# A planned issue order for the output projection and the second layer's input

## Chip, cores and metric

One core of a Trainium2 chip. The metric is the device time of one execution in microseconds (us); lower is better.

## What is computed

Two layers over 256 context rows and 1024 latent rows of width 1024 (1280 rows, ten tiles of 128). Layer 0 is a state-space mixer, layer 1 attention. The change lies at the end of layer 0 and the start of layer 1:

```python
def finish(y, xs, z):
    ...
    return rmsnorm(y * jax.nn.silu(z), norm_w) @ out_w      # 2048 -> 1024
...
h_lat = h_lat + gt[:, None] * o_lat
h_ctx = h_ctx + gtc * o_ctx
...
in_lat = rmsnorm(h_lat, norm_w[i]) * (1.0 + scl[:, None]) + sh[:, None]   # next layer
```

All is float32. A matmul is made of three, with each operand split into a high part that TensorE takes as it is and a low part that is the remainder.

## The kernel before

The kernel runs in stages. The first (the mixer's scans) and the last (attention) are issued by a `Plan`: the code hands it operations, each with its engine, a rank, a duration in us and the buffers that it takes (`hold`); `Plan.order` runs a list schedule over them (each engine takes, whenever it is free, the operation of lowest rank whose inputs and buffers are there), and the operations are then emitted in that order inside `tc.manual_schedule()`, which keeps it. Everything between is emitted in the order of its loops, and the framework's own scheduler, with its own model of time, decides each engine's queue. In the profile, instructions of a later part stand in the queues between those of an earlier one.

The stage of this change, called the output projection here, handles three blocks of token tiles, (0,4), (4,7) and (7,10). For each of 16 slices `kt` of the 2048 inner channels, a block does this:

- SP loads `yt` and `zt` from `y_d` and `z_d` (L1062, L1063; three slots each) and two halves of the weight slice `m_out_w` (L187; six raw slots in `workvv`, the first slice in the ring `wraw`).
- POOL multiplies them (L1064). ACT squares the product (L1068), POOL adds the squares to `acc` (L1069, a tile of `workkl`).
- ACT makes `yh` with the norm weight (L1072), DVE the remainder `yl` (L1073).
- ACT makes `whi` of each weight half (L180); the remainder `wlo` goes to POOL and DVE in turn (L182).
- PE makes six matmuls of 128x512 for each token tile into `po` (L164 to L166): 24 in a slice of block 0, 18 in one of the others. Block 0's first tile has the two `tr` banks of PSUM, all other tiles share the six `ob` banks.

After 16 slices `drain_tile` empties the banks (DVE L992, ACT L993, POOL L994). `closing` finishes the block while the next one runs, a step before each second slice: the sum of squares over channels (PE L1039), the inverse root (DVE L214, POOL L215), and for each token tile the residual sum (DVE L1000, input by SP L999, result to `h1_d` by L1002), its own norm (ACT L1004, L214, L215), the scaling by it (DVE L1007), eight transposes through the `tr` banks (PE L1015), and shift and scale with the split into the second layer's inputs `inh` and `inl` (ACT L1020 and L1026, DVE L1023 and L1027). Block 2's closing runs between the projections of the next stage, which takes it step by step.

What decides which engine makes a weight's remainder, and the order of the loops:

```python
self.n += 1
(G if self.n % 2 else V).tensor_tensor(lo, w, hi.bitcast(FT), op=OP.subtract)
...
for kt in range(16):
    if kt >= 2 and kt % 2 == 0:
        next(after, None)
```

Of the kernel before, what the change touches and what calls it, by code (L numbers as in the profile page):

```python
# [141 lines left out]
def emit(tc, A, out):  # L142
# [92 lines left out]
    def psum(tag, shape):  # L235
        return PS.tile(shape, FT, tag=tag, bufs=PSN[tag], name=tag)
# [735 lines left out]
    with ExitStack() as st:  # L972
# [5 lines left out]
        turn = [-1]  # L978

        def piece():  # L980
            turn[0] += 1
            return raw6[turn[0] % 6]


        rt1 = work[1][0:4, 4]
        inh, inl = both_parts()
        R2 = Ring(S2, 1, 4)

        def drain_tile(t, po):
            h1 = work[0][:, t % 5]  # L990
            g = gts[1 if t < 2 else 0]
            V.tensor_tensor(h1[:, 0:512], po[0], g[:, 0:512], op=OP.mult)  # L992
            S.activation(h1[:, 512:], po[1], AF.Copy)  # L993
            G.tensor_tensor(h1[:, 512:], h1[:, 512:], g[:, 512:], op=OP.mult)  # L994
            return h1

        def residual(t, h1, rstd):
            xt = work[1][:, t % 2]
# [8 lines left out]
            V.tensor_scalar(xt, h1, r, None, op0=OP.mult)  # L1007
            return xt

        def next_input(t, xt):  # L1010
            j = 1 if t < 2 else 0
            for h in range(2):
                p = psum("tr", [128, 4, 128])
                for i in range(4):
                    T.transpose(p[:, i, :], xt[:, (h * 4 + i) * 128:(h * 4 + i + 1) * 128], ident)  # L1015
                w = work[1][:, 2, h * 512:(h + 1) * 512].rearrange("p (a b) -> p a b", a=4)
                for i in range(4):
                    kt = h * 4 + i
                    if i % 2:
                        S.activation(w[:, i], p[:, i], AF.Identity, bias=shcol[1][:, kt, j:j + 1],  # L1020
                                     scale=gcol[1][:, kt, j:j + 1])
                    else:
                        V.tensor_scalar(w[:, i], p[:, i], gcol[1][:, kt, j:j + 1], shcol[1][:, kt, j:j + 1],  # L1023
                                        op0=OP.mult, op1=OP.add)
                ih = inh[:, h * 4:h * 4 + 4, t * 128:(t + 1) * 128]
                S.activation(ih, w, AF.Copy)  # L1026
                V.tensor_tensor(inl[:, h * 4:h * 4 + 4, t * 128:(t + 1) * 128], w, ih.bitcast(FT), op=OP.subtract)  # L1027

        def closing(b0, b1, h1s, acc):

            if b0 == 0:
                c = psum("tr", [128, KT, 4])
                for kt in range(KT):
                    T.transpose(c[:, kt, :], rt1[:, kt * 128:(kt + 1) * 128], ident[0:4, 0:4])
                mod_cols(1, c[:, :, 0:2], c[:, :, 2:4])
            ssq = M2.tile([128, 4], FT, tag="ssy", bufs=2, name="ssy")
            pss = psum("tr", [128, 4])
            for t in range(b0, b1):
                T.matmul(pss[:, t - b0:t - b0 + 1], acc[:, (t - b0) * 128:(t - b0 + 1) * 128], ones[:, 0:1],  # L1039
                         start=True, stop=True)  # L1040
            V.tensor_copy(ssq[:, :b1 - b0], pss[:, :b1 - b0])
            r = rsq(M2, ssq[:, :b1 - b0], 2 * D, "rsy", 2)
            yield
            xn = None
            for t in range(b0, b1 + 1):
                nxt = residual(t, h1s[t], r[:, t - b0:t - b0 + 1]) if t < b1 else None
                if xn is not None:
                    next_input(t - 1, xn)
                xn = nxt
                yield  # L1050

        after = iter(())
        for b0, b1 in ((0, 4), (4, 7), (7, 10)):
            n = (b1 - b0) * 128
            po = {(t, h): psum("ob" if b1 - t < 4 else "tr", [128, 512]) for t in range(b0, b1) for h in range(2)}
            acc = work[1][:, 3, (b0 == 4) * 512:((b0 == 4) + 1) * 512]
            for kt in range(16):
                if kt >= 2 and kt % 2 == 0:
                    next(after, None)
                yt = S2.tile([128, 512], FT, tag=f"yt{(b0 + b0 // 7 + kt) % 3}", bufs=1, name="yt")  # L1060
                zt = S2.tile([128, 512], FT, tag=f"zt{(b0 + b0 // 7 + kt) % 3}", bufs=1, name="zt")
                Q.dma_start(yt[:, :n], y_d[kt, :, b0 * 128:b1 * 128])  # L1062
                Q.dma_start(zt[:, :n], z_d[kt, :, b0 * 128:b1 * 128])  # L1063
                G.tensor_tensor(yt[:, :n], yt[:, :n], zt[:, :n], op=OP.mult)  # L1064
                if kt == 0:
                    S.activation(acc[:, :n], yt[:, :n], AF.Square)
                else:
                    S.activation(zt[:, :n], yt[:, :n], AF.Square)  # L1068
                    G.tensor_tensor(acc[:, :n], acc[:, :n], zt[:, :n], op=OP.add)  # L1069
                yh = S2.tile([128, 512], FR, tag=f"yh{(b0 + b0 // 7 + kt) % 3}", bufs=1, name="yh")  # L1070
                yl = S2.tile([128, 512], FR, tag=f"yl{(b0 + b0 // 7 + kt) % 3}", bufs=1, name="yl")
                S.activation(yh[:, :n], yt[:, :n], AF.Copy, scale=mnw[:, kt:kt + 1])  # L1072
                V.scalar_tensor_tensor(yl[:, :n], yt[:, :n], mnw[:, kt:kt + 1], yh[:, :n].bitcast(FT), op0=OP.mult,  # L1073
                                       op1=OP.subtract)
                if b0 == 0 and kt == 6:
                    for i in range(2):
                        Q.dma_start(rt1[2 * i:2 * i + 2], m_d[:, (i + 1) * 1024:(i + 2) * 1024])
                    for j in range(2):
                        Q.dma_start(gts[j], rows(m_d[j, 0:1024], 128))
                w = [(R2 if kt % 2 and b0 + kt > 1 else WR).load(A["m_out_w"][kt * 128:(kt + 1) * 128, h * 512:(h + 1) * 512],  # L1080
                                                                      piece() if b0 + kt else None)
                     for h in range(2)]
                for t in range(b0, b1):
                    k = slice((t - b0) * 128, (t - b0 + 1) * 128)
                    for h in range(2):
                        mm3(po[t, h], yh[:, k], yl[:, k], w[h][0], w[h][1], kt == 0, kt == 15)
            h1s = {t: drain_tile(t, [po[t, 0], po[t, 1]]) for t in range(b0, b1)}
            for _ in after:
                pass
            after = closing(b0, b1, h1s, acc)  # L1090

# [592 lines left out]
```

## Time and profile before

| | |
|---|---|
| time, median of 3 runs | 2061.88 us (2059.1 to 2063.29) |
| profiled execution | 2048.25 us, span 2046.1 us |
| PE busy | 1970.3 us, 96% of the span |
| DVE, ACT, POOL busy | 69%, 53%, 58% |
| granted TensorE clock, mean | 0.993 |
| output projection | 1025.12 to 1284.54 us of the span |

Engines: PE is TensorE, PEld its weight loads, DVE VectorE, ACT ScalarE, POOL GpSimd, SP SyncE (SPq its queue of DMA issues). A busy share is over the whole span; the stage has its own.

### The profile page before, as it was taken

Reading aid. Unit: us, or ns where it says so; the run is one execution under the profiler, and the core shown is the slowest. Engines: PE = TensorE matmul, PEld = TensorE weight load, DVE = VectorE, ACT = ScalarE, POOL = GpSimd, SP = SyncE. Lnnn points to the kernel's source line nnn. Section 1 sums busy time; section 2 is a strip of 40 time slices with the busy share of each in tenths; the row PEclk is TensorE's granted clock in tenths of the full one; section 3 lists DMA queues with packets and bytes.
Section 4 is the critical chain, followed back from the end, with each engine's and each line's share of the span. In section 5 each row is a group of like instructions: output and inputs, shape, how many; then the busy total and the mean of one; then the engine's idle time right before and its main releaser. Section 6 shows DMA issues by size and latency. Waiting matters only on the chain. (4 is left out here: it accounts for less than half of the span.)

```text
span 2046.1 us, 31950 instructions
## 1 busy us (share of the span) xinstructions
PE 1970.3 (96%) x11352; PEld 1533.5 (75%) x11352; DVE 1411.4 (69%) x1718; ACT 1082.3 (53%) x2004; POOL 1187.8 (58%) x977
## 2 busy tenths in 40 slices
PE   8899999999999999999998989999999999999998
PEld 8778888878887888788876777999786444444476
DVE  1495887787869695866354777755763888888653
ACT  2547768576766767576544555522223445454521
POOL 1202766666657574846287888753443666776722
PEclk9999999999999999999999999999999999999999
DMA  6115555435453546364585665451222011111023
GB/s 240 63 32 142 145 153 166 140 116 165 125 168 98 165 115 183 104 172 141 187 277 165 203 209 180 142 147 32 81 77 92 32 37 42 42 44 41 6 98 108
DMA packets 159699, 249.29 MB, mean 122 GB/s; under 512 B 22106, under 2 KB 57818, under 8 KB 159540
## 3 DMA queue, kind: packets, MB, share of 16 engines
q1 hardware_dynamic: 159252, 246.73, 39.1%
q8 instruction: 89, 1.46, 0.3%
q14 instruction: 70, 0.57, 0.1%
q10 hardware_dynamic: 288, 0.52, 0.1%
HBM read 204.49 MB, written 42.63 MB: 121 GB/s over the span
## 5 line engine op out<-in xcount | busy, mean ns | idle before, releaser
L164 PE MATMUL pj<-inh,whi 128*128 128x512 f32 (+1 forms) x1152 | 439.7, 382 | 3.9 <-DVE dv L449 3.2
L165 PE MATMUL pj<-inl,whi 128*128 128x512 f32 (+1 forms) x1152 | 408.8, 355 | 0.8 <-POOL inl L363 0.8
L166 PE MATMUL pj<-inh,wlo 128*128 128x512 f32 (+1 forms) x1152 | 409.6, 356 | 0.0
L750 POOL TENSOR_SCALAR_AFFINE_SELECT lab<-lab 128x512 f32<-128x512 f32 x160 | 146.6, 923 | 179.7 <-DMA lab<-la_d 168.2
L641 DVE SCALAR_TENSOR_TENSOR acc<-ub,convw,acc 128x1282 f32<-128x1282 f32 x128 | 232.1, 1813 | 18.7 <-ACT acc L638 15.7
L164 PEld LDWEIGHTS pj<-inh,whi 128*128 128x128 f32 x1152 | 218.3, 189 | 33.5 <-DVE dv L449 3.6
L166 PEld LDWEIGHTS pj<-inh,wlo 128*128 128x128 f32 x1152 | 217.5, 189 | 32.1
L165 PEld LDWEIGHTS pj<-inl,whi 128*128 128x128 f32 x1152 | 218.5, 190 | 26.3 <-POOL inl L363 1.2
L1428 POOL TENSOR_TENSOR acc<-acc,P 128x1024 f32<-128x1024 f32 x80 | 192.7, 2408 | 64.9 <-ACT P L1452 63.4
L1452 ACT ACTIVATE P<-sc 128x1024 f32<-128x1024 f32 x160 | 162.9, 1025 | 117.4 <-PE sc L1447 107.5
L756 ACT ACTIVATE W<-lab,u_t 128x128 f32<-128x128 f32 x640 | 201.4, 390 | 36.7 <-POOL lab L750 29.5
L1393 DVE TENSOR_REDUCE mx<-sc 128x2 f32<-128x1024 f32 (+1 forms) x140 | 167.3, 1213 | 55.5 <-PE sc L1272 54.5
L709 POOL TENSOR_TENSOR xw<-xst,te_t 128x256 f32<-128x256 f32 x144 | 141.9, 1002 | 42.4 <-DVE xst L693 16.5
L1463 PE MATMUL ot<-P,vv 128*64 128x512 f32 x640 | 154.7, 605 | 0.0
L1447 PE MATMUL sc<-q,kh 64*128 64x512 f32 x640 | 136.2, 421 | 1.2 <-ACT P L1452 0.9
L598 POOL TENSOR_TENSOR wlo<-wraw,whi 128x512 fp32r<-128x512 f32 x48 | 70.4, 1466 | 107.5 <-ACT whi L595 107.5
L164 PE MATMUL ob<-whi,inh 128*128 128x256 f32 x416 | 119.7, 289 | 3.3 <-DVE mx L1309 3.3
L164 PE MATMUL ob<-whi,yh 128*128 128x512 f32 x288 | 115.5, 405 | 6.5 <-DVE workkh L992 6.5
L166 PE MATMUL ob<-whi,inl 128*128 128x256 f32 x416 | 117.9, 284 | 0.0
L165 PE MATMUL ob<-wlo,inh 128*128 128x256 f32 x416 | 117.8, 284 | 0.0
L166 PE MATMUL ob<-whi,yl 128*128 128x512 f32 x288 | 115.4, 401 | 2.3 <-DVE yl L1073 2.3
L165 PE MATMUL ob<-wlo,yh 128*128 128x512 f32 x288 | 115.4, 401 | 0.0
(275 smaller groups left out, 4576.1 us busy)
## 6 DMA issues: line engine op xcount, KB each, us to landing
lab<-la_d SPq DMA_DIRECT2D x160, 256.0 KB
wraw<-in_w_in SPq DMA_DIRECT2D x96, 256.0 KB
workvv<-in_m_out_w SPq DMA_DIRECT2D x94, 256.0 KB
mraw<-in_mod_w SPq DMA_DIRECT2D x64, 256.0 KB
es<-e_d SPq DMA_DIRECT2D x128, 128.0 KB
spare<-in_mod_w SPq DMA_DIRECT2D x32, 256.0 KB
z_d<-zs SPq DMA_DIRECT2D x32, 256.0 KB
q_d<-qs SPq DMA_DIRECT2D x128, 64.0 KB
```

The costliest lines, as they stand in the source:

```text
L164: T.matmul(o, lh, rh, start=first, stop=False)
L165: T.matmul(o, lh, rl, start=False, stop=False)
L166: T.matmul(o, ll, rh, start=False, stop=last)
L641: V.scalar_tensor_tensor(t["a"], ub[i % 2][:, k:k + CW], convw[:, ct, k:k + 1], t["a"], op0=OP.mult, op1=OP.add)
L709: G.tensor_tensor(t[d], s["xst"][:, c], te_t[:, d, c, h4][:, :, None].to_broadcast([128, 4, 64]), op=OP.mult)
L750: G.affine_select(t["l", d], t["l", d], [[0, 4], [sgn, 128]], OP.is_ge, NEVER, base=0, channel_multiplier=-sgn)
L756: S.activation(t["w", d][:, h], t["l", d][:, h], AF.Exp, bias=u_t[:, d, c, 4 * g + h:4 * g + h + 1])
L1393: V.tensor_reduce(max_place(t["m"][0], i), o, AX.X, OP.max)
L1428: E.tensor_tensor(t[e], t["P", k0] if two else t[e], t["P", kt], op=OP.add)
L1447: T.matmul(o[:, h], (first_row[r] if n == 3 else (kh, kl, kh)[n][r, kv, k]), x[(0, 0, 1, 2)[n]][r], start=(n == 0), stop=(n == 3))
L1452: S.activation(t["P", kt], flat(t["s", kt]), AF.Exp)
L1463: T.matmul(t["o"][h * 64:(h + 1) * 64], vv[:, kt, kv], t["P", kt][:, h * 512:(h + 1) * 512], start=(kt == 0), stop=(kt == NT - 1))
```

## The change

Each operation of the output projection and of the closings of blocks 0 and 1 becomes an operation of a `Plan`, and the whole is emitted inside `tc.manual_schedule()`. Ranks are 1000 for a block and 20 for a slice; loads stand 45 to 50 below their slice, drains 700 below, the sum of squares 400 below; a closing's token tiles stand 60 apart from the next block's start. Block 2's closing stays as it was. The engines of three things change: of the weights' remainders POOL makes half in block 0, as before, and a quarter in blocks 1 and 2 (half before), DVE the rest; and in the planned closings the scaling by the norm goes from DVE to ACT. One PE operation is the six matmuls of a token tile in a slice, and it waits for both weight halves.

```diff
-ANY = ("tc", "wparts", "pj", "sc", "dn")
+ANY = ("tc", "wparts", "pj", "sc", "dn", "tr")
...
+        rings = {n + str(i): 1 for n, k in (("y", 3), ("yh", 3), ("raw", 6), ("h1", 5), ("x2", 2), ("w", 2)) for i in range(k)}
+        plan = Plan({**rings, "wa": 4, "wb": 4, "ob": 6, "tr": 2})
...
+            a = plan.op("SP", bring, [], R - 45, takes=raws)
+            a = plan.op("ACT", high, [a], R - 30, .63, takes=[parts], uses=raws)
+            pool = n % (2 if b == 0 else 4) == 1
+            return t, parts, plan.op(*(("POOL", lambda: low(G), [a], R - 30, 1.6) if pool else ("DVE", lambda: low(V), [a], R - 30, 1.2)),
+                                     uses=[*raws, parts])
...
+            a = plan.op("SP", bring, [], R - 50, us=.76, takes=[hy], move=2 * MOVE)
+            a = plan.op("POOL", lambda: G.tensor_tensor(t["yt"], t["yt"], t["zt"], op=OP.mult), [a], R - 40, 1.47 if wide else 1.27, uses=[hy])
+            h = plan.op("ACT", high, [a], R - 35, .71 if wide else .6, takes=[hh], uses=[hy])
+            l = plan.op("DVE", low, [h], R - 35, 1.3 if wide else 1.1, uses=[hy, hh])
...
+                    last[t] = plan.op("PE", product, [last.get(t), ly] + [w[2] for w in ws], R + t - b0, 1.38, takes=[] if kt else bs,
+                                      uses=bs + [hh] + [w[1] for w in ws])
...
+                a = plan.op("SP", bring, [], R - 60, takes=[hx], move=1.75)
+                a = plan.op("DVE", plus, [a, root] + done, R, 1.74, uses=[hx, hold])
...
+                a = plan.op("ACT", lambda x=x, xt=xt, h1=h1: S.activation(xt, h1, AF.Copy, scale=x["r"]), [a], R, 1.05, uses=[hx, hold])
...
+                    c = plan.op("PE", turn, [a], R, .44, takes=[bank], uses=[hx])
...
+        products(0)
+        context_rows()
+        products(1)
+        closing(0)
+        products(2)
+        closing(1)
+        with tc.manual_schedule():
+            for f in plan.order():
+                f()
```

## Rows read from the trace of the kernel before

**Rows 1.** Blocks 0 to 2: busy PE, PEld, DVE, ACT, POOL; clock, DMA share, GB/s.
```profile
1025.12:1114.45 89.33, 88.93 (x385) 71.79 (x383) 40.88 (x35) 39.18 (x69) 71.40 (x52) 1.00 0.70 230
1114.45:1206.25 91.80, 76.23 (x344) 62.24 (x343) 67.76 (x80) 51.33 (x102) 72.64 (x58) 0.94 0.64 199
1206.25:1284.54 78.29, 74.38 (x315) 59.54 (x315) 57.34 (x64) 43.38 (x86) 65.66 (x51) 0.94 0.58 186
```
**Rows 2.** Timeline of PE: start, us, instruction, count, idle time before it.
```profile
1025.12 0.40 PE L164 MATMUL tr<-whi,yh 128*128 128x512 f32 x1
...
1026.51 0.40 PE L164 MATMUL ob<-whi,yh 128*128 128x512 f32 x1
...
1030.47 0.40 PE L166 MATMUL ob<-whi,yl 128*128 128x512 f32 x1
...
1116.05 0.66 PE L1034 MATMUL tr<-ident,workkl 4*128 4x4 f32 x8 [1.45 <-DVE workkh L992]
...
1171.22 1.97 PE L1015 MATMUL tr<-ident,workkl 128*128 128x128 f32 x8 [2.50 <-ACT workkl L1020]
...
1206.25 0.77 PE L164 MATMUL ob<-whi,yh 128*128 128x512 f32 x1 [4.27 <-DVE workkh L992]
...
1258.61 1.09 PE L1015 MATMUL tr<-ident,workkl 128*128 128x128 f32 x8 [1.09 <-ACT workkl L1020]
```
**Rows 3.** Groups by line and shape, blocks 1 and 2: busy us, mean ns, idle before.
```profile
L182 POOL TENSOR_TENSOR wlo<-workvv,whi 128x512 fp32r<-128x512 f32 x30 | 50.0, 1666 | 0.0
L182 DVE TENSOR_TENSOR wlo<-workvv,whi 128x512 fp32r<-128x512 f32 x31 | 38.9, 1256 | 0.0
...
L1007 DVE TENSOR_SCALAR workkl<-workkh,rsq 128x1024 f32<-128x1024 f32 x7 | 9.9, 1409 | 3.7 <-POOL rsq L215 3.6
...
L1004 ACT ACTIVATE workkl<-workkh 128x1024 f32<-128x1024 f32 x7 | 7.4, 1058 | 6.1 <-DVE workkh L1000 6.1
...
L215 POOL TENSOR_TENSOR rsq<-rsq,mhalf 128x1 f32<-128x1 f32 x7 | 4.8, 692 | 4.8 <-DVE rsq L214 4.8
```
**Rows 4.** Single lines of DVE and POOL, blocks 1 and 2: shortest/median/longest ns.
```profile
L182 DVE TENSOR_TENSOR wlo<-workvv,whi x31: 676/1426/1783, 1113.9 to 1274.8; 128x512 fp32r<-128x512 f32 x31
...
L1073 DVE SCALAR_TENSOR_TENSOR yl<-yt,mnw,yh x31: 604/1306/1669, 1119.1 to 1276.5; 128x384 fp32r<-128x384 f32 x31
L1000 DVE SCALAR_TENSOR_TENSOR workkh<-workkh,rsq,workkl x7: 1284/2025/2043, 1137.9 to 1247.0; 128x1024 f32<-128x1024 f32 x7
L1007 DVE TENSOR_SCALAR workkl<-workkh,rsq x7: 742/1494/1778, 1144.8 to 1253.3; 128x1024 f32<-128x1024 f32 x7
L1027 DVE TENSOR_TENSOR inl<-workkl,inh x14: 683/692/1778, 1161.0 to 1269.3; 128x512 fp32r<-128x512 f32 x14
L182 POOL TENSOR_TENSOR wlo<-workvv,whi x30: 1263/1727/2286, 1117.9 to 1274.4; 128x512 fp32r<-128x512 f32 x30
...
L1064 POOL TENSOR_TENSOR yt<-yt,zt x29: 992/1325/2012, 1117.0 to 1270.5; 128x384 f32<-128x384 f32 x29
L1069 POOL TENSOR_TENSOR workkl<-workkl,zt x29: 987/1017/1463, 1113.4 to 1273.4; 128x384 f32<-128x384 f32 x29
L994 POOL TENSOR_TENSOR workkh<-workkh,gts x9: 1275/1438/1802, 1120.1 to 1284.3; 128x512 f32<-128x512 f32 x9
```
**Rows 5.** Timeline of SP's queue at the stage's start.
```profile
1015.23 0.41 SPq L1062 DMA_DIRECT2D yt<-y_d  x1
...
1026.39 0.32 SPq L659 DMA_DIRECT2D z_d<-zs  x1
...
1027.24 0.92 SPq L187 DMA_DIRECT2D workvv<-in_m_out_w  x2
```
**Rows 6.** Timelines of POOL, DVE and ACT in the same stretch.
```profile
1020.21 4.40 POOL L1064 TENSOR_TENSOR yt<-yt,zt 128x512 f32<-128x512 f32 x3 [8.31 <-DMA zt<-z_d]
...
1022.29 1.16 DVE L1073 SCALAR_TENSOR_TENSOR yl<-yt,mnw,yh 128x512 fp32r<-128x512 f32 x1 [7.90 <-ACT yh L1072]
...
1030.59 0.63 ACT L180 ACTIVATE whi<-workvv 128x512 fp32r<-128x512 f32 x1 [3.70 <-DMA workvv<-in_m_out_w]
```

More of the change, by code (lines that the diff above doesn't have):

```diff
@@ new lines, in emit, with context_rows, turn @@
+        BLK2 = ((0, 4), (4, 7), (7, 10))
+        Z, rows_in, cols_in = {}, [], []
+        def context_rows():
+            a = [plan.op("SP", lambda i=i: Q.dma_start(rt1[2 * i:2 * i + 2], m_d[:, (i + 1) * 1024:(i + 2) * 1024]), [], 125, small=True)
+                 for i in range(2)]
+            gs = [plan.op("SP", lambda j=j: Q.dma_start(gts[j], rows(m_d[j, 0:1024], 128)), [], 126, move=1.75) for j in range(2)]
+            hold, t = plan.hold("tr"), {}
+            def turn():
+                t["p"] = psum("tr", [128, KT, 4])
+                for kt in range(KT):
+                    T.transpose(t["p"][:, kt, :], rt1[:, kt * 128:(kt + 1) * 128], ident[0:4, 0:4])
+            rows_in.extend(gs)
+            b = plan.op("PE", turn, a, 990, .6, takes=[hold])
+            cols_in.append(plan.op("DVE", lambda: mod_cols(1, t["p"][:, :, 0:2], t["p"][:, :, 2:4]), [b], 1000, .5, uses=[hold]))
@@ new lines, in products, with product, left, right @@
+        def products(b):
+            b0, b1 = BLK2[b]
+            banks = {(t, h): plan.hold("ob" if b1 - t < 4 else "tr") for t in range(b0, b1) for h in range(2)}
+            po, last = {}, {}
+            for kt in range(16):
+                R = 1000 * b + 20 * kt
+                y, hh, ly = gated(b, kt, R)
+                ws = [weights(b, kt, h, R) for h in range(2)]
+                for t in range(b0, b1):
+                    def product(t=t, kt=kt, y=y, ws=ws):
+                        k = slice((t - b0) * 128, (t - b0 + 1) * 128)
+                        for h in range(2):
+                            if not kt:
+                                po[t, h] = psum("ob" if b1 - t < 4 else "tr", [128, 512])
+                            w = ws[h][0]
+                            mm3(po[t, h], y["h"][:, k], y["l"][:, k], w["hi"], w["lo"], kt == 0, kt == 15)
+                    bs = [banks[t, h] for h in range(2)]
+                    last[t] = plan.op("PE", product, [last.get(t), ly] + [w[2] for w in ws], R + t - b0, 1.38, takes=[] if kt else bs,
+                                      uses=bs + [hh] + [w[1] for w in ws])
+            for t in range(b0, b1):
+                h1, hold = work[0][:, t % 5], plan.hold(f"h1{t % 5}")
+                g = gts[1 if t < 2 else 0]
+                R = 1000 * b + 320 + t
+                def left(t=t, h1=h1, g=g):
+                    V.tensor_tensor(h1[:, 0:512], po[t, 0], g[:, 0:512], op=OP.mult)
+                def right(t=t, h1=h1):
+                    S.activation(h1[:, 512:], po[t, 1], AF.Copy)
+                a = plan.op("DVE", left, [last[t]] + rows_in, R - 700, .68, takes=[hold], uses=[banks[t, 0]])
+                c = plan.op("ACT", right, [last[t]], R - 700, .6, uses=[banks[t, 1], hold])
+                c = plan.op("POOL", lambda h1=h1, g=g: G.tensor_tensor(h1[:, 512:], h1[:, 512:], g[:, 512:], op=OP.mult), [c] + rows_in, R - 700,
+                            1.46, uses=[hold])
+                Z["h1", t] = (h1, hold, [a, c])
@@ L1029, in closing, with turn_half @@
[L1029 to L1035, printed above, removed]
+        def turn_half(t, xt, h):
+            p = psum("tr", [128, 4, 128])
+            for i in range(4):
+                T.transpose(p[:, i, :], xt[:, (h * 4 + i) * 128:(h * 4 + i + 1) * 128], ident)
+            return p
@@ L1036, in closing, with last_closing @@
+        products(0)
[7 more added lines that the diff above has]
+                f()
+        def last_closing():
+            b0, b1 = BLK2[2]
             ssq = M2.tile([128, 4], FT, tag="ssy", bufs=2, name="ssy")
             pss = psum("tr", [128, 4])
-            for t in range(b0, b1):
-                T.matmul(pss[:, t - b0:t - b0 + 1], acc[:, (t - b0) * 128:(t - b0 + 1) * 128], ones[:, 0:1],
-                         start=True, stop=True)
+            sums(2, pss)
@@ L1049, in closing @@
                 xn = nxt
                 yield
[L1052 to L1090, printed above, removed]
```

139 lines of the change are left out of this document (108 added, 31 removed).

## The prediction, made before the run

> **What bounds the kernel now.** I read the table of busy time by stretch first, cut at the three blocks. PE is the engine that sets the end of this stage, and blocks 1 and 2 are where it stands idle: 88.93 us busy of 89.33 in block 0, but 76.23 of 91.80 and 74.38 of 78.29 in the others, at a mean granted clock of 0.94 against 1.00 [rows 1]. What the stage needs at least follows from PE's timeline. The matmuls from the one at 1026.51 to the one at 1030.47 are 18, evenly spaced, so one takes 3.96 / 17 = 0.233 us at full clock [rows 2]. Block 0 has 16 x 24 = 384 matmuls, 89.5 us: as long as it took, nothing to win. Blocks 1 and 2 have 288 each, 67.1 us. Eight transposes of a token tile take 1.09 us [rows 2]; with four tiles in block 1, three in block 2, and about 0.6 us of small matmuls, the floors are 72.1 and 71.0 us. So block 1 loses 19.7 us and block 2 7.3 us: 27 us in all, and this is the most that better order can give here, unless the floor itself falls, for which the change has nothing.
>
> What makes the loss is seen next in the same timeline. Ten times PE's idle time in blocks 1 and 2 ends with a wait that the view names, the first at 1116.05, the last at 1258.61, 19.5 us together [rows 2]. Two kinds lead. At the turn of a block the first product waits for DVE to empty a bank (4.27 us at 1206.25), behind other work in DVE's queue. And eight transposes stand in PE's queue ahead of products that are ready, while ACT has not yet brought their input (2.50 us at 1171.22). Both are matters of order, not of an engine that is full. The rest of the 27 us, 7.5, is slow matmuls behind the gaps (the clock's 0.94) and small delays.
>
> **The change, part by part.** The matmuls, their shapes and the bytes moved are the same. Three things differ: the order in all queues, two moves between engines, and the seam to the stage before.
>
> The moves. In blocks 1 and 2, 64 weight halves have a remainder; POOL made 32 of them and will make 16. By the means of now POOL loses 16 x 1.666 = 26.7 us of its 72.64 + 65.66 = 138.3, which leaves 111.6; DVE gains 16 x 1.256 = 20.1. Seven scalings go from DVE (7 x 1.409 = 9.9) to ACT, where a pass over 1024 columns takes 1.058: 7.4 us [rows 1, 3]. DVE comes to 67.76 + 57.34 + 20.1 - 9.9 = 135.3 us, ACT to 51.33 + 43.38 + 7.4 = 102.1. Against PE's floor of 143.1 that is 95% for DVE, 78% for POOL, 71% for ACT. POOL is relieved, and DVE becomes the engine next to PE.
>
> So the order can't give all 27 us. I bound the new length of blocks 1 and 2 from both sides. Below: PE's floor, 143.1. Above: DVE and POOL hold each other up, which the trace shows. The same subtraction takes DVE between 676 and 1783 ns, POOL between 1263 and 2286 [rows 4]. If their work could not overlap at all, the sum of the shortest durations would be the floor. Now, POOL has 29 x 0.992 + 29 x 0.987 + 30 x 1.263 + 9 x 1.275 + 4.8 = 111.6; DVE, for operations of SBUF on SBUF, 31 x 0.676 + 31 x 0.604 + 7 x 1.284 + 7 x 0.742 + 14 x 0.683 = 63.5 [rows 3, 4]; together 175.1 us in the 170.1 us that blocks 1 and 2 took. They do overlap, then, but little. The change takes 16 x 1.263 + 7 x 0.742 = 25.4 off and puts 16 x 0.676 = 10.8 on: 160.5. In the same proportion (170.1 / 175.1) that is 155.9 us, if the pair was the limit all the time; but the kernel of now has stretches where PE's order was. I take 153, nearer to the upper end, since DVE has to reach 88% where it reaches 74% today. **Gain: 17 us**, between 14 and 27.
>
> The skill has a rule against this move. The Trainium skill, "SBUF — State Buffer", section "Who interferes with whom", says that a DVE operation with two SBUF inputs and a GpSimd operation that reads SBUF exclude each other, and the second "fully blocks". By that rule blocks 1 and 2 could not be shorter than the 160.5 us of shortest durations, and the gain would be at most 9.6; the trace has 175.1 us of such work in 170.1, so it agrees that they hardly overlap but not that they never do.
>
> The seam. In the kernel before, a `yt` load is issued at 1015.23, ahead of the last store of the stage before at 1026.39 in the same queue [rows 5]: the scheduler slips later work between. Now both stages are emitted in an order that is kept. No row shows two such stages in a row. If the second may still slip into the first's pauses, the start is about as before, with one difference: the raw slots in `workvv` get their first load at 1027.24, and `whi` of it starts at 1030.59 [rows 5, 6]. A product now waits for both halves. Two of ACT's 0.63 us and one POOL remainder of 1.3 to 1.7 end at 1033.2 to 1033.6. Slice 0 on PE, 24 x 0.233 = 5.6 us from 1025.12, ends at 1030.7. PE waits 2.5 to 2.9 us there, for 0.4 to 0.6 before. **Cost: 3 us** with a slow clock behind it. If it may not slip in, everything starts behind the store at 1026.39. From the load at 1015.23 to the end of the first `yl` at 1022.29 + 1.16 = 1023.45 are 8.2 us [rows 5, 6]. The load goes out at 1026.39 + 0.4, PE then starts at 1026.8 + 8.2 = 1035.0 instead of 1025.1: 9.9 us. I take 3, the case that the rows are nearest to, and keep 10 as the other end.
>
> The rest costs nothing, each for a reason. The drains get a rank 700 below, so they go first on DVE, ACT and POOL, and the same operations are done. Loads are the same; the DMA share was 0.58 to 0.70, and a stage shorter by a tenth brings it to about 0.68 (0.64 x 91.80 + 0.58 x 78.29 over 153) in blocks 1 and 2, below the 0.70 at which block 0 ran PE at 99% [rows 1]; if that cover were gone, each slice's y and z would be late, which the slower case below holds. Block 0 keeps half of the remainders on POOL and has PE as its bound. Block 2's closing and the next stage are as before.
>
> Sum: -17 + 3 = -14 us. The profiled execution of before is 2048.25 with a span of 2046.1, so the span would become about 2032. The three runs have a median of 2061.88, 13.6 us above the profiled one, a difference that has nothing to do with this stage; I put the change on the median: **2061.88 - 14 = 2048 us**.
>
> **The rivals.** *Late start.* The same gain of 17 us, but the seam costs 10: 2055 us. For it: both regions keep their order. Against: the scheduler does slip later work into the first region's pauses now.
>
> *The pair of DVE and POOL is the bound.* Blocks 1 and 2 take the 160.5 us of the sum of shortest durations, and with waits in fixed queues some 165: gain 5, seam 3, so 2060 us, no change. For it: 175.1 us of shortest work in 170.1. Against: PE's ten gaps were ended by order.
>
> *Slower: DVE becomes the limit, at contended durations.* With 48 instead of 32 remainders, DVE meets POOL more often. If the remainders' mean goes from 1.256 to the longest of now, 1.783, and the 32 `yl` from their median of 1.306 to their longest, 1.669, DVE needs 135.3 + 48 x 0.527 + 32 x 0.363 = 172.2 us [rows 3, 4], 2 more than both blocks take now; with the seam that is +5, 2067 us. It decides from a mean remainder of about 1.7 us. Against it: POOL, the other side, has a fifth less to do.
>
> *The order is better than I think.* DVE's durations fall as POOL is relieved, PE runs at its floor: gain 25, seam 3, 2040 us.
>
> **How the numbers follow.** Chances: my forecast (gain of 8 to 20 net) 0.48, late start 0.21, pair-bound 0.13, slower 0.10, better 0.08. The range takes in the late start and the better case, and on the slow side the pair-bound case: 2037 to 2061. The measurement tells 0.2%, some 4 us, from no change. Faster by more: forecast, better case and nearly all of late start, 0.76. Within: most of pair-bound and a little of late start, 0.13. Slower: 0.11.
>
> **What would show it.** Right: blocks 1 and 2 at 148 to 157 us, clock 0.97 or more; no gap above 1.5 us before the first product of a block or before transposes; DVE at 85 to 92% there, POOL near 75%; DVE's mean remainder still below 1.35 us. The seam: the first `yt` load before or behind the last store of L659, and PE's first idle time in the stage. Wrong, if PE's waits move to `yl` or `wlo` of DVE all along both blocks, if block 0 is longer than 93 us, or if the next stage starts with idle PE because its weights were not slipped into the planned queues.

## The result and the profile after

The change makes the kernel faster: a median of 2030.8 us (2027.88 to 2034.82, 4 runs) against 2060.49 (2054.57 to 2063.29, 4 runs) for the kernel before, a ratio of 0.9861 with an interval of 0.9832 to 0.989. The forecast was 2048 with a range of 2037 to 2061: the sign was right, the gain about twice the forecast, the time below the range. The profiled execution of after took 2029.27 us, its span 2027.5.

**By block.** The three blocks after, in the columns of [rows 1]:

```profile
1026.45:1119.03 92.58, 89.55 (x385) 71.81 (x384) 46.21 (x42) 44.44 (x78) 77.56 (x56) 1.00 0.75 244
1119.03:1191.10 72.07, 72.07 (x344) 59.51 (x342) 64.40 (x78) 53.47 (x102) 56.25 (x44) 1.00 0.73 236
1191.10:1262.78 71.68, 69.84 (x315) 56.39 (x314) 63.66 (x67) 46.88 (x88) 58.83 (x46) 1.00 0.64 207
```

Read it against [rows 1]. Block 0 is 3.3 us longer (92.58 for 89.33). Block 1 fell from 91.80 to 72.07, with PE busy for all of it; block 2 from 78.29 to 71.68. Blocks 1 and 2 together take 143.75 us, against a floor of 143.1 in the prediction. DVE is busy for (64.40 + 63.66) / 143.75 = 89% of that, POOL for (56.25 + 58.83) / 143.75 = 80%. So full a DVE hardly keeps PE waiting, as the next views show.

**PE's timeline** after: the turn to block 1, and all rows of the stage with a named idle time (in brackets: idle before, and what ended it).

```profile
1032.56 0.50 PE L164 MATMUL tr<-whi,yh 128*128 128x512 f32 x1 [0.36 <-ACT yh L1046]
1033.85 0.50 PE L166 MATMUL tr<-whi,yl 128*128 128x512 f32 x1 [0.56 <-DVE yl L1049]
...
1046.35 0.50 PE L164 MATMUL tr<-whi,yh 128*128 128x512 f32 x1 [1.55 <-ACT yh L1046]
1047.65 0.50 PE L166 MATMUL tr<-whi,yl 128*128 128x512 f32 x1 [0.56 <-DVE yl L1049]
...
1119.03 0.95 PE L1138 MATMUL tr<-ones,workkl 128*128 128x1 f32 x8
1119.91 0.66 PE L999 MATMUL tr<-ident,workkl 4*128 4x4 f32 x8
1120.50 0.50 PE L164 MATMUL ob<-whi,yh 128*128 128x512 f32 x1
...
1201.46 0.50 PE L166 MATMUL ob<-whi,yl 128*128 128x512 f32 x1 [1.36 <-DVE yl L1049]
...
1224.98 0.50 PE L166 MATMUL ob<-whi,yl 128*128 128x512 f32 x1 [0.48 <-DVE rsq L1180]
```

At the turn the first product (1120.50) follows the small matmuls without a gap, where [rows 2] had 1.45 us at 1116.05 and 4.27 at 1206.25. No transposes wait. What is left is 0.36 + 0.56 + 1.55 + 0.56 = 3.0 us at the stage's start, in slices 1 and 3, and 1.84 us in blocks 1 and 2, where the prediction counted 19.5.

**What PE waited for** in blocks 1 and 2, the view of waits: engine, line, releaser; us in total, times, longest. The kernel before:

```profile
PE ob L164 <- DVE workkh L992: 6.5, 2, 4.3
PE tr L1015 <- ACT workkl L1020: 5.9, 4, 2.5
PE tr L1039 <- ACT workkh L993: 3.4, 1, 3.4
...
PE tr L1034 <- DVE workkh L992: 1.4, 1, 1.4
```

The kernel after, the whole answer:

```profile
PE ob L166 <- DVE yl L1049: 1.4, 1, 1.4
PE ob L166 <- DVE rsq L1180: 0.5, 1, 0.5
```

The drains (L992, L993) are behind 6.5 + 3.4 + 1.4 = 11.3 us of the waits before, ACT's L1020 ahead of the transposes (L1015) behind 5.9. Both kinds are gone.

L1020 does not make the transposes' input, as the prediction reads it. It shifts and scales what the transposes of the tile before left in `tr`, so the next eight wait for the banks. Of the wait that ends at 1171.22, the kernel before:

```profile
1165.89 1.50 DVE L1007 TENSOR_SCALAR workkl<-workkh,rsq 128x1024 f32<-128x1024 f32 x1 [1.64 <-POOL rsq L215]
...
1170.71 0.81 ACT L1020 ACTIVATE workkl<-tr,shcol,gcol 128x128 f32<-128x128 f32 x2 [1.15 <-DVE workkl L1023]
```

The input was there at 1165.89 + 1.50 = 1167.39. ACT emptied the banks late, because its steps alternate with DVE's (L1023), and these (at 1167.31, 1168.60 and 1170.28) stood in DVE's queue among `yl` and `wlo`. It is still a matter of order, but of DVE's queue as much as of PE's.

**DVE's own waits** show the same from the side of the queue. Before, the three largest of 41 us with a named releaser:

```profile
DVE yl L1073 <- ACT yh L1072: 7.5, 6, 3.1
DVE workkh L1000 <- DMA workkl<-in_x: 6.2, 3, 2.9
DVE workkh L1000 <- POOL rsq L215: 5.4, 2, 4.5
```

After, the two largest of 16 us:

```profile
DVE workkl L1126 <- ACT workkl L1124: 7.2, 13, 1.2
DVE workkh L1091 <- PE ob L166: 6.5, 4, 4.5
```

Before, DVE stood for up to 4.5 us in front of one late operation, with everything behind it in its queue. After, what it waits for is mostly the end of a block's products (L1091, the longest of 4.5 us ahead of block 2's last ones) and the short modulation steps (L1126).

**The split work.** Groups by line after, blocks 1 and 2, columns as in [rows 3]:

```profile
L1021 DVE TENSOR_TENSOR wlo<-workvv,whi 128x512 fp32r<-128x512 f32 x44 | 56.8, 1318 | 0.5 <-ACT whi L1018 0.3 <-DMA workvv<-in_m_out_w 0.2
L1021 POOL TENSOR_TENSOR wlo<-workvv,whi 128x512 fp32r<-128x512 f32 x15 | 24.2, 1615 | 7.6 <-ACT whi L1018 7.6
...
L1189 ACT ACTIVATE workkl<-workkh,rsq 128x1024 f32<-128x1024 f32 x7 | 8.0, 1147 | 1.3 <-POOL rsq L1188 1.3
```

DVE's mean remainder went from 1256 to 1318 ns, below the 1.35 us given as the sign of a right forecast. A scaling on ACT takes 1147 ns, estimated at 1058.

**SP's queue at the seam**, to be read beside [rows 5]:

```profile
1016.61 0.40 SPq L1041 DMA_DIRECT2D yt<-y_d  x1
...
1027.33 0.33 SPq L659 DMA_DIRECT2D z_d<-zs  x1
1027.70 0.91 SPq L1013 DMA_DIRECT2D workvv<-in_m_out_w  x2
```

The stage's `yt` load is issued at 1016.61, ahead of the last store of the stage before at 1027.33. Two stages, each with its order kept, do interleave, and the late start that the prediction feared did not come.

### The profile page after: what moved, and what is told of

Its sections match the earlier page's. It is cut to its first block, busy times and chain, and to the rows that moved or that the text cites. A ratio compares the mean times of both kernels' runs of the same rounds, so it can differ in the third digit from the quotient of the medians.

```text
span 2027.5 us, 31896 instructions
## 1 busy us (share of the span) xinstructions
PE 1967.1 (97%) x11352; PEld 1532.1 (76%) x11352; DVE 1420.4 (70%) x1727; ACT 1092.3 (54%) x2011; POOL 1176.6 (58%) x961
## 4 chain that ended last, share of the span: by engine, by line
PE 75%; DVE 9%; DMA 6%; POOL 3%; issue 3%; ACT 2%; SPq 1%; DVEq 0%; POOLq 0%; ACTq 0%
PE pj L164 8%; PE pj L165 8%; PE pj L166 8%; PE sc L1591 7%; PE ot L1607 7%; PE ob L164 6%; PE ob L166 6%; PE ob L165 5%; DVE acc L641 3%; PE st L714 3%; PE yo L828 2%; PE sc L1416 2%; PE yd L787 2%; PE sc L166 1%; PE sc L164 1%
## 5 line engine op out<-in xcount | busy, mean ns | idle before, releaser
L165 PEld LDWEIGHTS pj<-inl,whi 128*128 128x128 f32 x1152 | 219.3, 190 | 26.5 <-POOL inl L363 1.2
L1591 PEld LDWEIGHTS sc<-q,kh 64*128 64x128 f32 x640 | 60.1, 184 | 70.6 <-DVE mx L1537 29.4
```

Of the source, the lines that this page charges most:

```text
L165: T.matmul(o, lh, rl, start=False, stop=False)
L1591: T.matmul(o[:, h], (first_row[r] if n == 3 else (kh, kl, kh)[n][r, kv, k]), x[(0, 0, 1, 2)[n]][r], start=(n == 0), stop=(n == 3))
```

## The experiments

The table goes by PE's timeline: the stage from its first product, cut where PE has done with the products of block 0 and of block 2. [rows 1] ends 0.16 us later, so the 169.9 us here are the prediction's 170.1. All in us of one profiled execution.

| kernel | stage starts | block 0 | blocks 1, 2 | stage | behind it | span |
|---|---|---|---|---|---|---|
| before | 1025.12 | 89.3 | 169.9 | 259.3 | 761.7 | 2046.1 |
| before again | 1029.11 | 89.4 | 168.5 | 257.9 | 768.5 | 2055.5 |
| moves alone | 1032.25 | 89.0 | 173.5 | 262.5 | 766.3 | 2061.0 |
| order alone | 1032.18 | 93.6 | 151.8 | 245.4 | 765.1 | 2042.7 |
| scaling on DVE | 1027.55 | 92.6 | 147.8 | 240.4 | 766.1 | 2034.0 |
| no remainder on POOL | 1033.76 | 92.3 | 145.8 | 238.1 | 765.0 | 2036.9 |
| after | 1026.45 | 92.6 | 143.75 | 236.3 | 764.7 | 2027.5 |
| after again | 1030.39 | 94.2 | 143.8 | 238.0 | 762.6 | 2031.0 |
| drains ranked late | 1029.05 | 93.4 | 143.45 | 236.8 | 764.8 | 2030.7 |
| drains behind slice 1 | 1031.32 | 93.6 | 145.8 | 239.4 | 768.0 | 2038.7 |
| drains behind slice 2 | 1029.63 | 92.0 | 147.5 | 239.5 | 764.1 | 2033.2 |
| start told to the plan | 1028.46 | 99.0 | 143.8 | 242.8 | 765.8 | 2037.1 |
| ACT held at the start | 1026.01 | 94.8 | 143.9 | 238.8 | 763.4 | 2028.2 |

**1. The kernel before, unchanged**, profiled once more.

> The kernel before, unchanged, to see what varies between its executions. Theory 1 (the 29.7 us between the medians are the 23 us by which the stage is shorter plus differences between executions that lie outside the stage): a stage of 259 us again, whatever the time. Theory 2 (the kernel before loses more in the stage in its usual executions than in the profiled one): a stage of 265 us or more where the time is near 2060 us. Ratio 1.00 within 0.3%.

2057.95 us (10 runs) against 2057.05 (21 runs), ratio 1.0007 [0.9991, 1.0023]. The profiled span is 9.4 us longer than the one shown ahead of the prediction, and the stage is not where that lies: 4.0 us are ahead of it, 6.8 behind it, and the stage itself is 1.4 shorter. A stretch of the next stage, first of the execution before, then of this one (columns as in [rows 1]):

```profile
1350.00:1450.00 100.00, 96.78 (x726) 91.00 (x725) 62.61 (x156) 28.67 (x71) 41.92 (x54) 1.00 0.26 77
```

```profile
1350.00:1450.00 100.00, 94.99 (x698) 90.94 (x697) 56.71 (x139) 28.74 (x70) 40.51 (x51) 0.93 0.27 81
```

The same program has a mean clock of 1.00 in one execution and 0.93 in the other, and gets 698 matmuls done where it did 726 (its stage ends 2.6 us later, so the two stretches hold the same work but for its edges). The lower clock goes with a longer wait of PE at one place, first before, then in this run:

```profile
1378.40 0.44 PE L1167 MATMUL tr<-ident,xd 128*128 128x128 f32 x2 [1.21 <-DVE qs L1202]
```

```profile
1383.41 0.69 PE L1167 MATMUL tr<-ident,xd 128*128 128x128 f32 x2 [3.69 <-DVE qs L1202]
```

Behind the 1.21 us the clock stayed at 1.00; behind the 3.69 us it was 0.50 from 1384 to 1388 us. Why DVE is later there is not shown. So spans of this kernel differ by some us for reasons that have nothing to do with the stage; a change in the stage is better measured in the stage.

**2. The order alone**: half of the remainders stay on POOL, the scaling stays on DVE.

```diff
-            pool = n % (2 if b == 0 else 4) == 1
+            pool = n % 2 == 1
...
-                a = plan.op("ACT", lambda x=x, xt=xt, h1=h1: S.activation(xt, h1, AF.Copy, scale=x["r"]), [a], R, 1.05, uses=[hx, hold])
+                a = plan.op("DVE", lambda x=x, xt=xt, h1=h1: V.tensor_scalar(xt, h1, x["r"], None, op0=OP.mult), [a], R, 1.4, uses=[hx, hold])
```

> The plan, but POOL makes half of the remainders in all blocks and DVE scales by the norm, as before: order alone. If PE's waits were a matter of order, blocks 1 and 2 shrink to 146 to 154 us, with POOL at 90 to 95% and short waits, and the time gains 15 to 22 us. If DVE and POOL as a pair set the time, the 175 us of shortest durations are back and blocks 1 and 2 take 163 us or more: a gain under 8 us.

2044.37 us (6 runs), ratio 0.9933 [0.9908, 0.9958]: 13 us less, where 15 to 22 were expected, since block 0 is 4 us longer. Blocks 1 and 2 take 151.8 us, as expected from order and 17 to 18 less than before. In that stretch:

```profile
1125.74:1277.56 151.82, 143.89 (x655) 116.83 (x654) 131.42 (x137) 92.65 (x182) 140.96 (x105) 0.99 0.65 210
```

PE's waits there:

```profile
PE ob L166 <- DVE yl L1049: 7.0, 4, 2.9
PE tr L1118 <- DVE workkl L1189: 0.9, 1, 0.9
```

Neither drains nor ACT are in the list any more. POOL is busy 140.96 / 151.82 = 93% of the time, DVE 87%, and what PE waits for is the `yl` at the end of the chain of POOL's product, ACT and DVE (ACT's `yh` stood for POOL's products for 26.5 us of this stretch). With the order mended, POOL is nearly full.

**3. The moves alone**, in the scheduler's own order: POOL makes a quarter of the remainders in blocks 1 and 2, ACT the scaling.

```diff
-    def split(self, w):
+    def split(self, w, eng=None):
...
-            (G if self.n % 2 else V).tensor_tensor(lo, w, hi.bitcast(FT), op=OP.subtract)
+            (eng or (G if self.n % 2 else V)).tensor_tensor(lo, w, hi.bitcast(FT), op=OP.subtract)
...
+            if t < 7:
+                S.activation(xt, h1, AF.Copy, scale=r)
+            else:
+                V.tensor_scalar(xt, h1, r, None, op0=OP.mult)
...
-                                                                      piece() if b0 + kt else None)
+                                                                      piece() if b0 + kt else None,
+                                                                      None if b0 == 0 else (G if (kt * 2 + h) % 4 == 1 else V))
```

> The kernel before with the two moves alone: POOL makes a quarter of the remainders in blocks 1 and 2, and ACT scales by the norm in the closings of blocks 0 and 1. If order is what counts, PE's idle time ahead of transposes and at the turns of blocks stays and blocks 1 and 2 take 160 to 170 us: a gain of 0 to 8 us. If the pair of DVE and POOL is what counts: 14.6 us of shared work less, blocks 1 and 2 near 156 us, a gain of 12 to 15 us.

2062.26 us (10 runs), ratio 1.0018 [0.9997, 1.004]: no gain, and blocks 1 and 2 are 4 to 5 us longer in the profile (173.5), above both cases of the expectation.

```profile
1121.22:1294.70 173.48, 155.02 (x656) 123.75 (x656) 113.71 (x148) 101.71 (x195) 114.90 (x92) 0.92 0.58 187
```

PE's waits in the stretch, the largest:

```profile
PE ob L166 <- DVE rsq L214: 9.0, 4, 3.2
PE ob L164 <- DVE workkh L992: 8.0, 2, 4.1
```

And DVE's largest:

```profile
DVE wlo L182 <- ACT whi L180: 22.3, 12, 3.5
```

POOL is relieved (115 us for 138), and DVE has less busy time than before the change (113.7 for 125.1 in the two blocks of [rows 1]), yet PE waits longer. Both turns again have a gap ended by the drains. DVE now stands 22.3 us in front of remainders whose high part ACT has not made. The framework orders the queues anew once the work has moved, so this run is not the old order with other engines; it shows that the moves bring nothing where the order is not planned.

**4. No remainder on POOL** in blocks 1 and 2: DVE makes all 64.

```diff
-            pool = n % (2 if b == 0 else 4) == 1
+            pool = b == 0 and n % 2 == 1
```

> The changed kernel with all remainders of blocks 1 and 2 on DVE, none on POOL. If DVE has a limit of its own: 16 more at 1.0 to 1.25 us bring it from 130 to 146 to 150 us in 143, blocks 1 and 2 take 150 to 158 us, 5 to 12 us slower than the changed kernel. If the pair's shared work is the limit: 16 x 0.59 = 9.4 us of it less, and it is as fast as the changed kernel or faster.

2036.43 us (4 runs), ratio 0.9905 [0.9878, 0.9933]; blocks 1 and 2 take 145.8 us, 2 more than with a quarter on POOL: neither the 150 to 158 of a DVE at its limit nor as fast as after. The stretch, and the group of remainders:

```profile
1126.09:1271.86 145.77, 143.01 (x656) 115.42 (x655) 124.11 (x159) 100.36 (x189) 92.83 (x74) 1.00 0.69 219
...
L1021 DVE TENSOR_TENSOR wlo<-workvv,whi 128x512 fp32r<-128x512 f32 x58 | 60.2, 1061 | 0.0
```

DVE makes a quarter of the remainders more than after (58 in the group, for 44) and is busy less: 124.1 us, for 128.1 after. Its mean remainder fell from 1318 to 1061 ns as POOL's busy time went from 115 to 93. A DVE instruction's duration thus goes with what POOL has to do; run 5 takes the pair by itself.

**5. The pair by itself.** A kernel without the reference's work: 24 of the remainders' subtractions on DVE alone, 24 on POOL alone, then 48 on DVE and 40 on POOL at the same time, all 128x512.

```diff
+            for k in range(40):
+                G.tensor_tensor(gb[k % 4], w[k % 2], hi[k % 2].bitcast(FT), op=OP.subtract)
+            for k in range(48):
+                V.tensor_tensor(vb[k % 4], w[k % 2], hi[k % 2].bitcast(FT), op=OP.subtract)
```

> No part of the computation: 24 remainders of 128x512 on DVE alone, 24 on POOL alone, then 48 on DVE and 40 on POOL at the same time. If the shortest durations exclude each other, the common stretch takes 48 x 0.68 + 40 x 1.27 = 83 us or more. If a good part of each is not exclusive (as 160 us of such work in the 147 us of the changed kernel's blocks 1 and 2 suggests), it takes 60 to 72 us. With no conflict at all it takes 51 us, POOL's own time.

The timeline of both engines (start, busy us of the row, instruction, count):

```profile
4.11 14.67 DVE L162 TENSOR_TENSOR va<-w,hi 128x512 fp32r<-128x512 f32 x24 [4.11 <-ACT hi L159]
20.80 29.32 POOL L166 TENSOR_TENSOR ga<-w,hi 128x512 fp32r<-128x512 f32 x24
53.48 66.26 POOL L172 TENSOR_TENSOR gb<-w,hi 128x512 fp32r<-128x512 f32 x40
...
55.22 70.49 DVE L174 TENSOR_TENSOR vb<-w,hi 128x512 fp32r<-128x512 f32 x48
```

The durations by line, shortest/median/longest ns; for DVE in the common stretch the 39 that began while POOL still ran:

```profile
L162 DVE TENSOR_TENSOR va<-w,hi x24: 679/681/692, 4.1 to 18.1; 128x512 fp32r<-128x512 f32 x24
L166 POOL TENSOR_TENSOR ga<-w,hi x24: 1260/1262/1262, 20.8 to 48.9; 128x512 fp32r<-128x512 f32 x24
L172 POOL TENSOR_TENSOR gb<-w,hi x40: 1262/1703/1707, 53.5 to 118.0; 128x512 fp32r<-128x512 f32 x40
L174 DVE TENSOR_TENSOR vb<-w,hi x39: 1744/1744/1744, 55.2 to 118.5; 128x512 fp32r<-128x512 f32 x39
```

The common stretch takes 72.2 us (53.48 to 125.71), at the upper end of the middle case. Alone, a subtraction starts every 14.67 / 24 = 0.611 us on DVE and every 29.32 / 24 = 1.222 on POOL. Beside POOL, DVE's 39 begin within 118.55 - 55.22 = 63.33 us, one every 63.33 / 38 = 1.667, and each takes 1.744 us instead of 0.68; POOL keeps the same pace. The nine left over, behind POOL's last, take 0.68 again. A pair thus takes 1.67 us. The sum of the durations alone is 0.683 + 1.262 = 1.945, that of the spacings 1.833. The two slow each other down strongly, but the pair takes 0.86 of the sum of shortest durations, the sum that the prediction took for a near floor.

The Trainium skill, "SBUF — State Buffer", section "Who interferes with whom", calls the shared ports an exclusive lock; by that rule a pair could not take less than the sum. It takes 1.833 - 1.667 = 0.17 us less by the spacings, 0.28 by the durations: the measurement decides, the two instructions overlap little, but not by nothing. Which part of them overlaps is not shown.

**6. The drains ranked late**, behind the next block's first slices.

```diff
-                a = plan.op("DVE", left, [last[t]] + rows_in, R - 700, .68, takes=[hold], uses=[banks[t, 0]])
+                a = plan.op("DVE", left, [last[t]] + rows_in, R + 720, .68, takes=[hold], uses=[banks[t, 0]])
```

(and the same for ACT's and POOL's part)

> The changed kernel with the drains' rank 720 above their slice instead of 700 below, so that they queue behind the first slices of the next block. If the late drains made the gaps at the turns of blocks, gaps of 2 to 5 us come back there and the stage takes 241 to 248 us. If the gaps had another cause, the stage stays at 236 us.

2029.74 us (4 runs), ratio 0.9863 [0.9844, 0.9882]; blocks 1 and 2 at 143.45. Nothing changes. But the drains hardly moved: at the first turn DVE empties the `ob` banks from 1119.40 to 1122.65, ahead of block 1's first product at 1123.90. A rank is a preference only, and the plan takes a drain of high rank too where its engine is free. So this run does not test a late drain there. At the second turn they do stand behind two `yl` and a `wlo`, from 1195.21 to 1196.49, and PE's first product of block 2 (1196.42) has no wait.

**7. The start told to the plan**: its model holds the first products, and the loads of raw slots, for 10 us.

```diff
+        begin = plan.op("-", lambda: None, us=10.)
...
-            a = plan.op("SP", bring, [], R - 45, takes=raws)
+            a = plan.op("SP", bring, [begin] if raw else [], R - 45, takes=raws)
...
-                    last[t] = plan.op("PE", product, [last.get(t), ly] + [w[2] for w in ws], ...
+                    last[t] = plan.op("PE", product, [last.get(t) or begin, ly] + [w[2] for w in ws], ...
```

> The changed kernel, with the plan told that PE and the raw slots come free 10 us after its start, as the trace shows. If the 3.7 us of gaps in the first three slices come from ACT's queue, where the weights of slice 1 stand ahead of its yh, these gaps fall below 1.5 us and the stage takes 233 to 235 us; else 236.

2039.06 us (4 runs), ratio 0.9912 [0.9895, 0.9928], neither case of the expectation: worse than the change on the same chip (run 8, 2032.37), with 4.8 us more in block 0 (99.0 for 94.2). PE's one named gap there:

```profile
1041.69 0.79 PE L164 MATMUL tr<-whi,yh 128*128 128x512 f32 x1 [7.48 <-ACT whi L1019]
```

Held back, the weight loads came behind the loads of the modulation rows and gates in SP's queue: the first into `workvv` went out at 1033.37 instead of 1027.70, in a stage that starts 2.0 us later.

**8. The kernel after, unchanged**, on the chip of runs 5 to 7.

> The changed kernel, unchanged, for its spread: a stage of 235 to 238 us, the rest of the span differing by several us from the first profile, as between the two executions of the kernel before (if theory 1 holds); ratio 0.986 within 0.003.

2032.37 us (4 runs), ratio 0.988 [0.9861, 0.9898]. Blocks 1 and 2 repeat to 0.1 us (143.8); block 0 is 1.6 longer.

**9 and 10. The drains forced late**: DVE's part of block b's drains waits for `yl` of slice 1 of the next block, and in run 10 of slice 2.

```diff
+                if kt == 1:
+                    for o in Z.get(("left", b - 1), []):
+                        o.after.append(ly)
...
+                Z.setdefault(("left", b), []).append(a)
```

(with `kt == 2` in run 10)

> The changed kernel, but DVE empties the banks of blocks 0 and 1 only behind the yl of the next block's slice 1, as it stood in the queue before the change (there: two yl and a wlo ahead of the drain). If this place in the queue made the gaps at the turns, 2 to 5 us of idle PE come back at each of the two turns and the stage takes 241 to 247 us. If not, 236 to 238 us as in the changed kernel.

> The changed kernel with the drains of blocks 0 and 1 on DVE behind the yl of the next block's slice 2, which can't be made before PE has done with the last slice of the block (three yh slots). Behind slice 1, whose yl is ready early in the plan, they cost nothing at the first turn. If a drain costs when it stands behind work that is itself late (as before the change, where the yl ahead of it waited for ACT and POOL), gaps of 2 to 5 us come back at both turns and the stage takes 242 to 248 us. If the place in the queue does not matter, 236 to 240.

Run 9: 2035.78 us (4 runs), ratio 0.9898 [0.9867, 0.993], blocks 1 and 2 at 145.8. Run 10: 2036.55 (4 runs), 0.9905 [0.9874, 0.9936], at 147.5. The second turn of run 10 has a gap as long as the old one, but it ends with another wait, for ACT's `yh`, which stood 5.32 us for POOL's product:

```profile
1201.03 0.50 PE L164 MATMUL ob<-whi,yh 128*128 128x512 f32 x1 [4.24 <-ACT yh L1046]
```

The first turn has no gap in either. In run 9 the drains there were not late (1121.87 to 1125.12, block 1's first product at 1126.38). In run 10 DVE's first drain of an `ob` bank there starts only at 1125.15, and block 1's first product at 1122.45. The two kernels lose 2 and 4 us in blocks 1 and 2, not the 17 or 18 that the order gave, and no wait of PE there ends with a drain. That the drains' place by itself made the gaps of before is not shown.

**11. ACT held at the start**: the plan is told that ACT's high parts of slice 1's weights can't start before 14 us, and products not before 9.5.

```diff
+        begin, weights_in = [plan.op(e, lambda: None, us=u) for e, u in (("-", 9.5), ("--", 14.))]
...
-            a = plan.op("ACT", high, [a], R - 30, .63, takes=[parts], uses=raws)
+            a = plan.op("ACT", high, [a, weights_in] if n in (2, 3) else [a], R - 30, .63, takes=[parts], uses=raws)
```

(and the products' wait on `begin`, as in run 7)

> The changed kernel with one place of the plan told the truth: the weights of slice 1 can't be split before 14 us after the plan's start, so ACT makes the yh of slice 1 first; the first six loads keep their order. If ACT's queue makes the gaps of 1.3 to 1.5 us before slice 1, they go and the stage takes 234 to 236 us; the gap before slice 3 stays, since its load is late. If the loads make both, nothing changes.

2034.72 us (4 runs), ratio 0.9893 [0.9868, 0.9919]; block 0 at 94.8, no better. The small gaps of the start became one:

```profile
1037.19 0.51 PE L165 MATMUL tr<-wlo,yh 128*128 128x512 f32 x1 [4.51 <-POOL wlo L1022]
```

PE now waits for the remainder of slice 1's weights on POOL. ACT had made its high part by 1030.09 + 1.40 = 1031.49. But the plan also changed POOL's order: POOL multiplies slice 2's `yt` and `zt` first, and stands for their load:

```profile
1032.97 1.26 POOL L1053 TENSOR_TENSOR yt<-yt,zt 128x512 f32<-128x512 f32 x1 [6.14 <-DMA zt<-z_d]
```

The remainder starts at 1035.42. So the run does not separate ACT's order from the loads; what sets the seam's price stays open.

**12. The scaling back on DVE**, all else as after.

```diff
-                a = plan.op("ACT", lambda x=x, xt=xt, h1=h1: S.activation(xt, h1, AF.Copy, scale=x["r"]), [a], R, 1.05, uses=[hx, hold])
+                a = plan.op("DVE", lambda x=x, xt=xt, h1=h1: V.tensor_scalar(xt, h1, x["r"], None, op0=OP.mult), [a], R, 1.4, uses=[hx, hold])
```

> The changed kernel with the scaling by the norm on DVE, as before; POOL keeps its quarter of the remainders. If POOL's relief is what the second part of the gain (order alone has blocks 1 and 2 at 154.8 us, the change 146.7) comes from, this stays within 2 us of the changed kernel's stage. If DVE's load is, DVE at 137 us of 144 leaves no room and the stage takes 241 us or more.

2036.47 us (4 runs), ratio 0.9908 [0.9882, 0.9933]; blocks 1 and 2 at 147.8. (The expectation's 154.8 and 146.7 are 3 us above the table's 151.8 and 143.75; the difference is the same.) The stage takes 240.4 us, 4 more than after: closer to the case in which DVE's load counts.

```profile
1120.11:1267.91 147.80, 142.58 (x656) 115.66 (x655) 137.24 (x152) 91.95 (x182) 118.66 (x88) 1.00 0.67 215
```

DVE is 93% busy here, and every named wait of PE in the stretch is for DVE (`yl` 2.9 us, `wlo` 2.3). With run 2 this splits the gain: order 169.9 to 151.8, POOL's quarter to 147.8, the scaling on ACT to 143.75, that is 18, 4 and 4 us, taken in this order; the scaling was not moved by itself. Measured against the repeat of run 1 (168.5) the first term is 17.

## Why the predicted gain was too small

- **Block 0, nothing to win; the seam, 3 us.** The size is right, with luck; the reason holds in part. The start is 1.3 us later than before (1026.45 for 1025.12), within the 4 us by which the start of the unchanged kernel differs from run to run. Block 0 is 3.3 us longer (4.8 in the two repeats, 94.2 us, which is past the 93 that the prediction named as a sign of being wrong), with 3.0 us of gaps. At slice 1, for which the prediction has 2.5 to 2.9 us, they are 0.36 + 0.56 = 0.92, and they end with `yh` and `yl`, not with a weight: ACT stood in front of the late load, with `yh` (1031.80) behind it in its queue.

```profile
1030.56 1.34 ACT L1018 ACTIVATE whi<-workvv 128x512 fp32r<-128x512 f32 x2 [2.74 <-DMA workvv<-in_m_out_w]
```

  The other 2.1 us stand at slice 3, of which the prediction has nothing; there ACT stood 5.10 us for a load, until 1044.37, again with `yh` behind it. The other end, 10 us, fell with the `yt` load ahead of the stores.
- **Where PE loses time, and that at most 27 us are there.** Right. Both kinds of wait vanished, the clock is 1.00, and 26.2 of the 27 us came back. What the transposes waited for was misread: banks that ACT and DVE had yet to empty, not their input. The next stage starts without idle PE, as the prediction had it (49.87 of its first 50 us busy).
- **DVE next to PE, POOL relieved.** Right in kind: DVE 89%, forecast as 85 to 92, POOL 80%, forecast as near 75. DVE's busy time is 128.1 us, where the prediction had 135.3 by the means of before. Nearly all of that difference is work that the plan does earlier, while block 0 still runs (DVE is busy for 46.21 us there, 40.88 before): blocks 1 and 2 hold 44 remainders for 31 + 16 = 47, 30 `yl` for 31 and 7 drains of DVE for 10, by the means of before 3 x 1.256 + 1.185 + 3 x 0.680 = 7.0 us. The means did not fall together: the remainder's rose from 1256 to 1318 ns, that of `yl` went from 1185 to 1092.
- **The step that failed** is the term of blocks 1 and 2: "I take 153, nearer to the upper end". Measured is 143.75. The upper end, 155.9, scaled the shortest durations by 170.1 / 175.1, the overlap that happened to be in the kernel before. But the pair was not the limit there. By run 5 a pair needs 0.86 of its durations' sum: 175.1 x 0.86 = 151 us of the 170, so the two engines had 19 us to spare, and for the changed kernel 160.5 x 0.86 = 138, below PE's floor. That is an estimate, since run 5 measured one kind of operation and blocks 1 and 2 have several. Run 2 fits it: the same work in a planned order took 151.8 us, with POOL 93% busy. The ratio of before was no property of the engines but of a kernel in which they waited. The rival in which the order is better (gain 25, seam 3) is what happened in size, given 8 in 100; the fall of DVE's durations that it names did not come.
- **The moves.** The prediction took them as part of one plan without a price for each. Without the order they give nothing (+3 to 5 us in the stage, a ratio of 1.0018 with an interval that holds 1); with it they give 8 (151.8 to 143.75). That is as the prediction's mechanism would have it: as long as order makes the gaps, an engine's share does not matter. The slower rival needed a mean remainder of about 1.7 us on DVE; it is 1.318. The DMA share in blocks 1 and 2 is 0.69, forecast 0.68, and no load of y, z or weights is late there for PE.
- **The base, and what lies outside the stage.** The time is 17.2 us below the forecast, and the failed step is only a part of that. The stage gave 26.2 - 3.3 = 23 us in the two profiles where 14 were forecast, 9 us of the miss; by itself this would have made 2061.88 - 23 = 2039 us, inside the range. 1.4 us are the base, 2060.49 for 2061.88. The other 29.7 - 23 = 6.7 us do not lie in the stage. They are fewer in the other sets: in run 8 the medians differ by 24.4 us, and the two repeats give 20 us in the stage; on the chips of the experiments the kernel before has medians of 2056.5 to 2058.8. What stands behind the stage varies between 761.7 and 768.5 us over all profiles, with either order, so the profiles do not show that the change did anything there. This remainder stays open.
- **Slips in the sums that change nothing.** DVE's shortest durations add up to 63.4 us, not 63.5. The slower rival raises `yl` from its median in a total that has it at its mean of 1.185: 176 us, not 172. A matmul of the first slice stands 0.233 us from the next, later ones 0.227 (13 within 1281.21 to 1284.15); PE's busy time in blocks 1 and 2 after is 141.91 us, so the floor of 143.1 was a little high.
- **Still open too**: which part of the order made the turns' gaps. The order as a whole is shown (run 2 against runs 1 and 3). Drains ranked late (run 6) were in time at the first turn, came later at the second and change nothing, the kernels with drains forced late on DVE (runs 9, 10) lose 2 to 4 us, and what stood ahead of the drains in DVE's queue before, and the order in which ACT and DVE empty the `tr` banks, were not tried one by one.

## What to carry to other kernels

Before an engine's busy time is taken as a floor, measure what it needs when nothing else is late: the durations in a trace contain the neighbours' share (0.68 us alone and 1.74 beside POOL for the same subtraction), and the overlap in a kernel full of waits is no limit. Count the operations in a stretch before and after as well: a planned order moves work across the cuts. Where most gaps of the bounding engine end with operations whose own engine has time to spare, a planned order can bring most of the gaps back (18 of 27 us here by itself, 26 with the moves), and the floor of the bounding engine is the first guess. Mend the order first, then move work: the same two moves were worth 8 us behind a good order and nothing ahead of it.

## What the runs showed of the hardware

- **A gap can cost more than its length.** In run 2 PE stood idle for 2.91 us up to 1212.12. The granted clock ahead of it and behind it:

```profile
1200.00:1208.00 8.00, 8.00 (x37) 6.58 (x37) 6.76 (x7) 4.28 (x9) 8.00 (x7) 1.00 0.62 204
1212.50:1215.00 2.50, 2.50 (x8) 1.91 (x7) 2.50 (x2) 1.77 (x4) 2.50 (x3) 0.50 0.98 353
```

  PE was busy throughout in the first stretch, at the upper level (2.4 GHz). Behind the gap it is at the lower one (1.2 GHz), and gives 8 matmuls in 2.5 us where it gave 37 in 8. This is part of the 7.5 us that no gap names: the mean clock of blocks 1 and 2 was 0.94 before and 1.00 after. Not every gap does it. At one place ahead of the stage PE stood idle for 3.18 us up to 110.98 in the kernel before, and the clock stayed at 1.00; in run 1, the same program, it stood there for 2.74 us up to 111.82, and the clock was 0.50 from 114 to 118 us.
- **DVE and POOL hold each other up, but not wholly**: one subtraction every 0.61 and 1.22 us alone, one of each every 1.67 us together (run 5). A remainder on DVE took 1061, 1318 and 1744 ns (means) with POOL busy for 64%, 80% and all of the time (run 4, after, the 39 of run 5 beside POOL).
- **The same program does not repeat itself** in stretches far from any change: mean clocks of 1.00 and 0.93 at 1350 to 1450 us, with a wait of PE for DVE of 1.21 and 3.69 us (run 1).
